# A four-sublayer decoder trunk on one core: the program is ordered by the scheduler's timeline simulation instead of its default one

## The chip, the cores and the metric

The kernel runs on one core of a Trainium2 chip. A core has five engines, each with its own queue, which it works off strictly in order: PE (TensorE: matrix multiplications; the load of its stationary operand is listed apart as PEld), DVE (VectorE: elementwise), ACT (ScalarE: elementwise with function tables), POOL (GpSimd) and SP (SyncE), which in this kernel issues all transfers between memory and the core. An engine that must wait for another waits on a semaphore, and everything behind that instruction in its queue waits too. The metric is the device time of one execution in microseconds (us).

## The reference

The reference does one inference step of a small hybrid decoder in fp32 for 512 prompt tokens and 64 sample tokens (8 sequences of 8), which share the weights. The model width is 1024. What is computed, cut to its core:

```
x += even_mixer(rmsnorm(x))   # conformer convolution + sliding-window attention (softmax with sinks)
x += conv_ffn(rmsnorm(x))     # silu(causal_conv3(h @ w_gate)) * (h @ w_up) @ w_down
x += odd_mixer(rmsnorm(x))    # Mamba-2: in-projection, conv4, chunked SSD scan, silu(z) gate, group RMS norm, out
x += conv_ffn(rmsnorm(x))
# the SSD scan of one head (32 heads in 4 groups, chunks of 128 tokens):
decay  = exp(where(causal, acum[l] - acum[s], -inf))
y_diag = ((C @ B.T) * decay * dt) @ x          # inside a chunk
states = B.T @ (decay_end * dt * x)            # what a chunk adds to the state
y_off  = (C @ h_prev) * exp(acum)              # what the earlier chunks bring
y = rmsnorm_group((y_diag + y_off + D * x) * silu(z)) @ w_out
```

The new states, caches and convolution histories are outputs too.

## The kernel before

The 576 tokens lie in the free dimension, in two halves of 288, with channels on the partitions. Every projection goes through `mm3` (lines 173 to 175): an fp32 product is made of three products of rounded parts (high by high, low by high, high by low), so each 128x128 block of weights against a half of the tokens costs three matrix multiplications of 288 columns. These three lines are 10,080 of the 11,007 multiplications that stand in PE's queue. Weights come in tiles of up to 1024 columns through rings of three buffers: the transfer lands in `wr`, ACT makes the rounded part `wh` (line 163), DVE the remainder `wl` (line 164).

The program goes through four sublayers in turn: `mix0` (convolution and attention), `ffn` 0, `mix1` (Mamba-2), `ffn` 1. In `mix1` the scan is written group by group as a generator `ssd(g)`, g = 0 to 3, and `run` weaves the projections of other parts between its steps, so that PE has multiplications (called **fillers** below) to do while a group's chains go from engine to engine. The chains of a group are:

- `xde` (DVE) to the state products `pst` (line 1081, PE; two pairs a group) to the states `hst` (lines 1087 to 1090), which free the two `xde` tiles of the pair.
- `decays(r)` for each of eight heads: the tile `acb` is loaded by SP (line 1112), goes through four Relu (line 1116) and one Exp (line 1117) on ACT and a multiplication by the mask on DVE (line 1118). The masks are forced into the order of the heads by a manual dependency.
- `outputs(t)` for four pairs of heads: 16 small multiplications `yp` (line 1148) take two `acb` tiles; `carried(t)` makes `py` (line 1133) for the same pair. DVE adds both into `xs` (lines 1152 and 1153).
- `begin`, `turn`, `finish`: the sample tokens, with `pyo` (line 1170) from loaded states `h0`, a transpose (line 1187), products `pst` (line 1200) and the outgoing states (lines 1203 and 1204).
- `gate(g)`: Silu of z (line 1262), products with it (1266), squares, the group norm through `rstd` (line 202: `pt`; a square root and DVE steps; line 218: `pr`), the scaling (1270) and the split into `yh`, `yl` (193, 194), on which the out-projection of the group works.

Tiles on the chip come from a list of 48 and later 59 slots (`S` and `free`). Which slot a tile gets is settled while the program is written down, in that order, and not by the scheduler. So an `acb` tile can only be loaded when the tile that had its slot before is done: in group 2, `acb_10552` takes the slot of `xde_10378` of the second state pair, `acb_10560` that of `hst_10415`, `acb_10680` that of `acb_10560`, `acb_10688` that of `ea2_10504`.

The order on each engine comes from the framework's scheduler. It simulates the program and, whenever a simulated engine comes free, gives it the instruction that it takes to be ready, earlier written ones first. A few places are bound by hand (`keep_in_program_order`, `issue_after`, the masks). The time at which the simulation believes an operand to be ready thus decides which of several waiting instructions goes ahead in a queue; on the chip the queue is then fixed.

## Time and profile before

| what | value |
|---|---|
| time, median of 3 runs | 1554.57 us (1550.0 to 1555.12) |
| the profiled execution's own time | 1553.1 us |
| its span in the profile | 1551.3 us |
| PE busy in the span | 1520.5 us (98%) |
| DVE, ACT, POOL busy | 1018.5, 649.3, 154.7 us |
| mean granted clock of PE | 0.997 of full speed |

The profile's page gives each engine's busy time, the longest chain of work, the groups of instructions by line, and the transfers. By time, `mix0` takes the first 195 us, `ffn` 0 until about 630 us, `mix1` until about 1,130 us (its groups end near 785, 905, 1,025 and 1,100 us), and `ffn` 1 the rest. A row of a timeline begins with the start in us and the duration in us; the bracket at its end gives the idle time before it and what ended it.

### The profile page before, as it was taken

The numbers are of one execution on the slowest core, as the hardware profiler recorded it, in microseconds if no ns is written. First come the engines' busy times: TensorE is split into PE (matmuls) and PEld (weight loads), VectorE is DVE, ScalarE is ACT, GpSimd is POOL, SyncE is SP. The second block draws the span as 40 slices with busy tenths as digits, with TensorE's granted clock in tenths as the row PEclk, the third lists the DMA queues.
The fourth block names the chain that finished last, engine by engine and source line by source line (L and its number), as shares of the span: only waits on it lengthen the run. The fifth ranks groups of instructions, "written<-read, shape, count | busy, mean of one in ns | idle before, by whom it ended". The sixth has DMA issues, their size and how long they took to land.

```text
span 1551.3 us, 28549 instructions
## 1 busy us (share of the span) xinstructions
PE 1520.5 (98%) x11635; PEld 1449.8 (93%) x11635; DVE 1018.5 (66%) x1805; ACT 649.3 (42%) x1232; POOL 154.7 (10%) x365
## 2 busy tenths in 40 slices
PE   8999999999999999999999999999999999999999
PEld 7977799999999999898988988998999999999999
DVE  7969887553555464678896786777976644663552
ACT  6356553221222222486855654646632222321220
POOL 0036001000000000011211112102010000000000
PEclk9999999999999999999999999999999999999999
DMA  8515223222222222136245245245222222223222
GB/s 239 136 42 131 85 70 98 86 86 85 83 77 78 92 82 85 55 104 202 71 148 180 83 115 185 72 125 173 87 84 85 91 83 82 82 73 92 82 87 75
DMA packets 69938, 157.80 MB, mean 102 GB/s; under 512 B 19871, under 2 KB 24607, under 8 KB 69807
## 3 DMA queue, kind: packets, MB, share of 16 engines
q1 hardware_dynamic: 69806, 155.97, 33.2%
q8 instruction: 92, 1.51, 0.4%
q14 instruction: 40, 0.32, 0.1%
HBM read 140.73 MB, written 15.21 MB: 101 GB/s over the span
## 4 chain that ended last, share of the span: by engine, by line
PE 88%; DVE 5%; ACT 4%; DMA 2%; issue 1%; SPq 0%; ACTq 0%; DVEq 0%
PE mm L173 27%; PE mm L175 27%; PE mm L174 26%; DMA acb<-acd 2%; PE yp L1148 1%; DVE wl L164 1%; ACT acb L1116 1%; PE mm L594 1%; ACT wh L163 1%; PE pst L1081 1%; PE pt L1063 1%; ACT sm L661 1%; PE py L1133 1%; PE pst L1200 1%; DMA out_ssm_s<-h 1%
## 5 line engine op out<-in xcount | busy, mean ns | idle before, releaser
L173 PE MATMUL mm<-hh,wh 128*128 128x288 f32 x2272 | 677.8, 299 | 6.8 <-ACT wh L163 5.5
L174 PE MATMUL mm<-hl,wh 128*128 128x288 f32 x2272 | 673.9, 297 | 0.7 <-DVE hl L389 0.4
L175 PE MATMUL mm<-hh,wl 128*128 128x288 f32 x2272 | 673.3, 297 | 0.5 <-DVE wl L164 0.4
L163 ACT ACTIVATE wh<-wr 128x1024 fp32r<-128x1024 f32 (+2 forms) x215 | 223.3, 1039 | 544.6 <-PE mm L174 275.1
L173 PEld LDWEIGHTS mm<-hh,wh 128*128 128x128 f32 x2272 | 428.3, 189 | 16.0 <-ACT wh L163 6.0
L174 PEld LDWEIGHTS mm<-hl,wh 128*128 128x128 f32 x2272 | 429.0, 189 | 4.8 <-issue 1.8
L175 PEld LDWEIGHTS mm<-hh,wl 128*128 128x128 f32 x2272 | 428.7, 189 | 3.2 <-issue 1.4
L164 DVE TENSOR_TENSOR wl<-wr,wh 128x1024 fp32r<-128x1024 f32 (+2 forms) x215 | 258.6, 1204 | 73.0 <-ACT wh L163 71.4
L173 PE MATMUL mm<-yh,wh 128*128 128x288 f32 x960 | 285.9, 298 | 1.5 <-DVE x L288 1.4
L175 PE MATMUL mm<-yh,wl 128*128 128x288 f32 x960 | 284.2, 297 | 1.3 <-DVE wl L164 1.3
L174 PE MATMUL mm<-yl,wh 128*128 128x288 f32 x960 | 285.3, 297 | 0.0
L173 PEld LDWEIGHTS mm<-yh,wh 128*128 128x128 f32 x960 | 181.1, 189 | 5.7 <-DVE x L288 2.5
L175 PEld LDWEIGHTS mm<-yh,wl 128*128 128x128 f32 x960 | 181.1, 189 | 2.4 <-DVE wl L164 1.6
L174 PEld LDWEIGHTS mm<-yl,wh 128*128 128x128 f32 x960 | 181.2, 189 | 1.5 <-issue 1.0
L288 DVE TENSOR_TENSOR x<-x,mm 128x288 f32<-128x288 f32 x192 | 84.9, 449 | 143.0 <-PE mm L175 142.8
L333 DVE TENSOR_TENSOR gbuf<-mm,rs 128x224 f32<-128x224 f32 x44 | 17.2, 391 | 108.6 <-PE mm L175 108.6
L344 ACT ACTIVATE gsilu<-gconv,par 128x512 f32<-128x512 f32 x44 | 31.8, 724 | 115.1 <-DVE gconv L341 115.1
L341 DVE SCALAR_TENSOR_TENSOR gconv<-gbuf,par,gconv 128x592 f32<-128x592 f32 x88 | 73.1, 831 | 1.5
L354 DVE TENSOR_TENSOR gsilu<-mm,gsilu 128x288 f32<-128x288 f32 x88 | 40.0, 454 | 50.5 <-PE mm L175 50.5
L880 DVE SCALAR_TENSOR_TENSOR cconv<-cbuf,par,cconv 128x600 f32<-128x600 f32 x72 | 59.6, 838 | 10.1 <-ACT cconv L878 9.5
L336 POOL COPY fpo<-gbuf 128x2 f32<-128x2 f32 x44 | 12.4, 281 | 476.0 <-DVE gbuf L333 476.0
L1116 ACT ACTIVATE acb<-acb,ac 128x128 f32<-128x128 f32 x128 | 41.4, 390 | 35.6 <-DMA acb<-acd 25.0
(322 smaller groups left out, 1593.6 us busy)
## 6 DMA issues: line engine op xcount, KB each, us to landing
wr<-in_w_gate SPq DMA_DIRECT2D x44, 512.0 KB, 3.5
wr<-in_w_up SPq DMA_DIRECT2D x44, 512.0 KB, 3.5
wr<-in_w_in_o SPq DMA_DIRECT2D x40, 512.0 KB, 3.6
wr<-in_w_down SPq DMA_DIRECT2D x32, 448.0 KB, 3.3
wr<-in_w_down SPq DMA_DIRECT2D x16, 512.0 KB, 3.5
h<-in_h SPq DMA_DIRECT2D x32, 256.0 KB, 3.1
acb<-acd SPq DMA_DIRECT2D x32, 256.0 KB, 4.2
out_ssm_s<-h SPq DMA_DIRECT2D x32, 256.0 KB, 2.6
```

What stands on the lines that cost most here:

```text
L163: nc.scalar.activation(hi[:, a:b], raw[:, a:b], AF.Copy)
L164: nc.vector.tensor_tensor(lo[:, a:b], raw[:, a:b], hi[:, a:b].bitcast(F32), op=SUB)
L173: nc.tensor.matmul(out, hi[:, ws], xh[:, sl], start=i == 0, stop=False)
L174: nc.tensor.matmul(out, hi[:, ws], xl[:, sl], start=False, stop=False)
L175: nc.tensor.matmul(out, lo[:, ws], xh[:, sl], start=False, stop=i == n - 1)
L288: nc.vector.tensor_tensor(self.x[m][:, sl], self.x[m][:, sl], p[:, :HB], op=ADD)
L333: nc.vector.tensor_tensor(g[:, 290:514], p[:, 0:224], rs[:, HB:NP], op=MUL)
L341: nc.vector.scalar_tensor_tensor(cv[:, :592], g[:, k:592 + k], w(k), cv[:, :592], op0=MUL, op1=ADD)
L344: nc.scalar.activation(sl[:, :NP], cv[:, :NP], AF.Silu, bias=b)
L354: nc.vector.tensor_tensor(sl[:, HALF[half]], p[:, :HB], sl[:, HALF[half]], op=MUL)
L880: nc.vector.scalar_tensor_tensor(cv[:, :600], g[:, k:600 + k], w(k), cv[:, :600], op0=MUL, op1=ADD)
L1116: nc.scalar.activation(acb[:, cs], acb[:, cs], AF.Relu, bias=ac[:, o:o + 1], scale=-1.0)
```

## The change

One argument is given where the program is traced. The scheduler then decides what is ready by its timeline simulation instead of its default one, for the whole program.

```
-    with tile.TileContext(nc) as tc:
+    with tile.TileContext(nc, schedule_with_timeline_sim=True) as tc:
         build(nc, tc, d)
```

The instructions of PE (11,007), DVE (1,807), POOL (370) and SP (436) are the same as before, with the same tiles in the same slots; ACT has 9 more, all of them loads of a function table (1,198 and 1,207 instructions). What changes is the order. `ffn` 0, `ffn` 1 and the end of the program are ordered nearly as before. The other parts are not. The table gives, for `mix1`, how many of the `mm3` multiplications stand ahead of an instruction in PE's queue, before and now. That is the measure in which the prediction counts fillers.

| | second `pst` pair (1081) | `yp` of the four pairs of heads | `pt`, `pt` / `pr`, `pr` of the group norm | out-projection begins |
|---|---|---|---|---|
| group 0 before | 4620 | 4608, 4656, 4704, 4752 | 4818, 4852 / 4865, 4915 | 4992 |
| group 0 now | 4728 | 4721, 4752, 4776, 4834 | 4944, 4974 / 4992, 4992 | 4992 |
| group 1 before | 5107 | 5132, 5174, 5225, 5280 | 5431 / 5468 (first ones) | 5664 |
| group 1 now | 5209 | 5226, 5280, 5301, 5328 | 5491 / 5515 (first ones) | 5664 |
| group 2 before | 5766 | 5798, 5835, 5883, 5952 | 6103 / 6140 (first ones) | 6336 |
| group 2 now | 5914 | 5928, 5952, 5971, 6029 | 6167 / 6195 (first ones) | 6336 |
| group 3 before | 6459 | 6528, 6575, 6592, 6605 | 6660, 6676 / 6678, 6714 | 6720 |
| group 3 now | 6564 | 6600, 6660, 6660, 6679 | 6720, 6720 / 6720, 6740 | 6720 |

In `mix0` the two `pt` and the two `pr` of the convolution's layer norm stood at 771 and 809, and 811 and 870, where the out-projection begins at 870; they stand at 849 and 859, and 864 and 866. Ahead of `mix1` the first `pr` of the norm (half 0) stood at 4210 and stands at 4224, where the first multiplication that needs it stands in both. At the very start ACT's first square (line 225) stands ahead of the first `wh` (line 163) and stood behind it. In group 3, SP loads the tiles of heads 4 to 7 ahead of those of heads 0 to 3, and the loads of `acb_11889` and `acb_11881`, on which the first `yp` waits, stand behind a load of weights (`wr_12607`) that stood after them.

First place: PE in group 2, just behind the second `yp`. (`py_10583` is the carried part of the third pair of heads, `pst_10628` and its like the sample's state products, `pyo` the sample's output from the loaded states `h0`, `mm` a filler.) Before:

```order
L1133 MATMUL py_10583<-cfm_9740,hst_10412 128x128
L1200 MATMUL pst_10629<-x3_10209,b3_10194 128x512
L173 MATMUL mm_10644<-yh_9645,wh_10590 128x288
L174 MATMUL mm_10644<-yl_9646,wh_10590 128x288
L175 MATMUL mm_10644<-yh_9645,wl_10591 128x288
L173 MATMUL mm_10644<-yh_9647,wh_10590 128x288
L174 MATMUL mm_10644<-yl_9648,wh_10590 128x288
L1200 MATMUL pst_10628<-x3_10209,b3_10194 128x512
```

Now:

```order
L1133 MATMUL py_10583<-cfm_9740,hst_10412 128x128
L1200 MATMUL pst_10629<-x3_10209,b3_10194 128x512
L1200 MATMUL pst_10628<-x3_10209,b3_10194 128x512
L1170 MATMUL pyo_10775<-h0_10678,cfm_9740 32x512
L1170 MATMUL pyo_10775<-h0_10676,cfm_9740 32x512
L1170 MATMUL pyo_10775<-h0_10674,cfm_9740 32x512
L1170 MATMUL pyo_10775<-h0_10672,cfm_9740 32x512
L1200 MATMUL pst_10636<-x3_10209,b3_10194 128x512
L1200 MATMUL pst_10637<-x3_10209,b3_10194 128x512
```

The fillers that stood between the small products have moved ahead of them, and `pyo_10775` has moved up; its `h0_10678` takes the slot of `acb_10552`, which the `yp` just before has read.

Second place: PE at the end of group 3, around the group norm and the start of the last out-projection (`mm_12453` to `mm_12481` are fillers of group 2's out-projection, `mm_12535` is the first product of group 3's, which needs `yh_12289` from the norm). Before:

```order
L174 MATMUL mm_12467<-yl_11029,wh_12449 128x288
L202 MATMUL pt_12357<-gssq_12287,o512_110 32x72 x4
L173 MATMUL mm_12481<-yh_11028,wh_12449 128x288
L174 MATMUL mm_12481<-yl_11029,wh_12449 128x288
L218 MATMUL pr_12328<-dg_12320,l1_75 128x288
L175 MATMUL mm_12453<-yh_11028,wl_12450 128x288
```

Now:

```order
L1133 MATMUL py_12118<-cfm_11125,hst_11778 128x128
L1133 MATMUL py_12118<-cfm_11125,hst_11780 128x128
L1133 MATMUL py_12118<-cfm_11125,hst_11850 128x128
L1187 MATMUL pt_12189<-ident_73,yo_12132 128x128 x4
L1200 MATMUL pst_12196<-x3_11604,b3_11585 128x512
L1200 MATMUL pst_12195<-x3_11604,b3_11585 128x512
L1200 MATMUL pst_12237<-x3_11604,b3_11585 128x512
L1200 MATMUL pst_12238<-x3_11604,b3_11585 128x512
L202 MATMUL pt_12315<-gssq_12287,o512_110 32x72 x4
L202 MATMUL pt_12357<-gssq_12287,o512_110 32x72 x4
L218 MATMUL pr_12328<-dg_12320,l1_75 128x288
L173 MATMUL mm_12535<-yh_12289,wh_12531 128x288
```

All fillers of group 2's out-projection now stand ahead of `py_12118`; behind it only the small products of the last group are left ahead of `mm_12535`.

Third place: ACT in `mix0`, where the softmax (line 661) alternates with the sigmoid of the convolution's gate (line 418). One piece of the difference:

```order
-L661 ACTIVATE sm,den<-sm,neg,rsq 128x128 x7
-L661 ACTIVATE sm,den<-sm,neg,rsq 128x256
+L661 ACTIVATE sm,den<-sm,neg,rsq 128x128 x5
+L418 ACT_TABLE_LOAD
+L418 ACTIVATE sg<-sg 128x288
+L163 ACTIVATE wh<-wr 128x1024
+L661 ACT_TABLE_LOAD
+L661 ACTIVATE sm,den<-sm,neg,rsq 128x256 x4
 L659 ACTIVATE es<-es 128x8
```

A sigmoid that stood behind the whole run of exponentials has moved into it, with a table load ahead of it and another one behind it. Over the part, the loads for these two lines go from 6 to 10.

## The prediction

> **What bounds the kernel now.** I read the page's head first, then the time by stages.
>
> ```profile
> span 1551.3 us, 28549 instructions
> PE 1520.5 (98%) x11635; PEld 1449.8 (93%) x11635; DVE 1018.5 (66%) x1805; ACT 649.3 (42%) x1232; POOL 154.7 (10%) x365
> 80.00:160.00 80.00, 77.64 (x649) 58.22 (x647) 62.38 (x178) 50.85 (x136) 38.42 (x39) 1.00 0.36 93
> 195.00:630.00 435.00, 435.00 (x3283) 434.24 (x3282) 242.32 (x398) 126.30 (x187) 17.82 (x83) 1.00 0.27 83
> 705.00:785.00 80.00, 79.25 (x618) 71.63 (x617) 68.61 (x117) 58.16 (x130) 17.49 (x32) 1.00 0.40 131
> 785.00:905.00 120.00, 115.31 (x887) 106.74 (x885) 90.71 (x151) 68.65 (x147) 19.83 (x33) 1.00 0.42 129
> 905.00:1025.00 120.00, 116.00 (x883) 107.64 (x882) 90.71 (x152) 69.36 (x148) 19.59 (x34) 0.99 0.41 127
> 1025.00:1095.00 70.00, 65.22 (x508) 57.07 (x509) 54.28 (x100) 40.25 (x89) 9.50 (x13) 1.00 0.46 142
> ```
>
> The window rows give length, then busy time and instructions of PE, PEld, DVE, ACT and POOL, the granted clock, and what the transfers did. PE is busy for 1520.5 of 1551.3 us. The change removes no multiplication, so no order can gain more than the 30.8 us in which PE is idle. In `ffn` 0 PE is never idle: 435.00 us over 3283 multiplications is 0.1325 us for a filler. In the groups of `mix1` the idle time is 0.75, 4.69, 4.00 and 4.78 us, 14.2 in all. Who ends it:
>
> ```profile
> PE yp L1148 <- DVE acb L1118: 7.2, 5, 2.4
> PE pst L1200 <- ACT ysb L1191: 1.9, 2, 1.3
> PE pr L218 <- DVE dg L214: 1.6, 3, 1.2
> PE mm L173 <- DVE x L288: 1.4, 2, 1.1
> ```
>
> (Us in total, times, longest.) So PE waits above all for the decay tiles. The kernel is fast because fillers cover chains through SP, ACT and DVE; the question is what the new order does to that cover.
>
> **The price of a chain.** Two waits of before, followed in time on PE:
>
> ```profile
> 920.44 1.91 PE L1081 MATMUL pst<-xde,btok 128*128 128x512 f32 x4
> 926.91 1.07 PE L1170 MATMUL pyo<-h,cfm 128*32 128x512 f32 x8
> 928.37 1.09 PE L1148 MATMUL yp<-acb,xdt 128*64 128x128 f32 x16
> 929.39 0.94 PE L1133 MATMUL py<-cfm,hst 128*128 128x128 f32 x6
> 934.70 0.60 PE L1187 MATMUL pt<-ident,yo 128*128 128x128 f32 x4
> 936.49 1.09 PE L1148 MATMUL yp<-acb,xdt 128*64 128x128 f32 x16 [0.80 <-DVE acb L1118]
> 948.21 1.97 PE L1148 MATMUL yp<-acb,xdt 128*64 128x128 f32 x16 [2.42 <-DVE acb L1118]
> ```
>
> These are group 2's second state pair and its first three `yp`. From the end of the state pair (922.35) to the second `yp` (936.49) are 14.1 us: **chain P2**, since its `acb` tiles take slots of that pair's `xde` and `hst`. From the end of the second `yp` (937.58) to the third (948.21) are 10.6 us: **chain P1**, since one tile takes the slot of the tile just read. Both are true lengths, because PE stood waiting at their ends. As a test of the counting: before, 48 fillers (6.4 us), `py` (0.9) and `pst` (1.5) stand between the second and third `yp`, which leaves a wait of 1.8 us; the row shows 2.42. Between pair and second `yp` stand 69 fillers (9.1) and 4.5 us of small products: a wait of 0.5 us by count; the row shows 0.80. What P1 is made of, the chain of waits shows for group 3:
>
> ```profile
> 1054.54 1.05 PE yp L1148 x16
> 1055.59 5.30 DMA acb<-acd
> 1061.00 1.57 ACT acb L1116 x5
> 1062.57 0.53 ACT acb L1117
> 1063.12 0.88 DVE acb L1118
> 1064.03 1.27 ACT acb L1116 x4
> 1066.37 1.09 DVE acb L1118
> 1067.50 1.09 PE yp L1148 x16
> ```
>
> There it takes 11.9 us. Moving fillers on PE shortens none of these pieces, except that the load of 5.30 us stood among others: the page gives
>
> ```profile
> acb<-acd SPq DMA_DIRECT2D x32, 256.0 KB, 4.2
> ```
>
> With 4.2 us P1 is 10.8. I take 10.6; the ends are 8 (an estimate: one tile alone, with the load of 4.2, four Relus of 1.27, an Exp of 0.6, the mask of 1.1 and the gaps between) and 12.
>
> **The change in `mix1`.** The state pairs now stand about 100 fillers later, and the four `yp` of a group closer together. A wait is the chain less what stands inside it on PE.
> - Group 0: from the state pairs (4728) to the second `yp` (4752) stand 24 fillers (3.2 us), the second pair (1.9), two `py` (1.8) and `pyo` (1.1), 8.0 with the rest of the first `yp`; P1 leaves 2.6. To the third `yp` (4776) 24 fillers (3.2) and 3.9 of small products leave 3.5. The fourth, 58 fillers on, has its cover. At 4992, where out-projection 0 begins, both `pr` now stand directly ahead of it, and what follows a `pr` is open (rows below): about 4. Sum 10.1.
> - Group 1: 71 fillers (9.4) and 4.6 of small products cover P2 (5209 to 5280). To the third `yp` 21 fillers (2.8) and 3.0 leave 4.8; the fourth 0.6. Sum 5.4.
> - Group 2: 38 fillers (5.0) and 4.6 leave 4.5 of P2 (5914 to 5952); to the third `yp` 19 fillers (2.5) and 3.0 leave 5.1 of P1; inside it also lies the wait of `pyo_10775` for its load. The fourth, 58 fillers on, is covered. Sum 9.6.
> - Group 3: the first `yp` stands 36 fillers (4.8) and 1.9 of small products behind the second pair. Its tiles take slots of `xde` tiles of both pairs, and their loads now stand behind a load of weights on SP: 7.4 by P2, 3.9 by P1; I take 7.4. The second `yp`, 60 fillers on (8.0 and `py`), waits 1.7. Then the norm. Its chain before, from DVE and ACT:
>
> ```profile
> 1078.64 0.75 DVE L1152 SCALAR_TENSOR_TENSOR xs<-xs,par,yp 128x512 f32<-128x512 f32 x1
> 1084.40 1.19 DVE L1266 TENSOR_TENSOR xs<-xs,zs 128x288 f32<-128x288 f32 x3
> 1087.56 1.28 ACT L209 ACT_TABLE_LOAD   x1
> 1088.85 0.32 ACT L209 ACTIVATE rv<-pt,eps 128x72 f32<-128x72 f32 x1
> 1091.50 0.45 DVE L214 TENSOR_TENSOR dg<-rv,rsc 128x288 fp32r<-128x288 f32 x1
> 1092.44 0.41 ACT L220 ACTIVATE grs<-pr 128x288 f32<-128x288 f32 x1 [0.46 <-PE pr L218]
> 1093.62 1.37 DVE L1270 SCALAR_TENSOR_TENSOR xs<-xs,par,grs 128x288 f32<-128x288 f32 x3
> 1094.16 1.30 ACT L193 ACTIVATE yh<-xs 128x288 fp32r<-128x288 f32 x3 [1.15 <-DVE xs L1270]
> ```
>
> From the products with z (1084.40) to the first `yh` (about 1094.6) are 10.2 us, from the last `yp`'s addition 16.0. Before, more than 100 fillers lay beside it; now none is left behind `py_12118`, whose sum into `xs` (1 us) comes ahead of that chain. I take 11, between 8 (only the last tile's products remain) and 16 (all of it). The step from `grs` to the third `yh` (1092.44 to 1095.46), 3 us a half, is also group 0's 4. Sum of group 3: 20.1.
>
> Together 45.2. The old waits on `yp` and `pst` (7.2 + 1.9 = 9.1) are what these replace: net **+36.1**.
>
> **The change elsewhere.**
> - Attention. ACT there, in three stretches, and what a table load costs:
>
> ```profile
> 100.00:110.00 10.00, 9.66 (x68) 7.96 (x67) 4.62 (x17) 9.45 (x27) 5.55 (x8) 1.00 0.00 0
> 110.00:120.00 10.00, 9.78 (x72) 8.62 (x71) 5.20 (x24) 9.07 (x23) 6.10 (x7) 1.00 0.26 68
> 120.00:130.00 10.00, 10.00 (x67) 7.66 (x64) 9.74 (x23) 8.70 (x27) 6.39 (x6) 1.00 0.72 188
> L418 ACT ACT_TABLE_LOAD x3 | 3.8, 1283 | 0.1
> 105.20 1.28 ACT L418 ACT_TABLE_LOAD   x1
> 106.49 0.78 ACT L418 ACTIVATE sg<-sg 128x288 f32<-128x288 f32 x2
> ```
>
> ACT is busy for 27.2 of 30 us and gets four more loads of 1.283 us: 5.1 on 2.8 of free time, so **+2.5**; 0 if PE's fillers cover the delay, 5.1 if ACT sets the pace. The other five of the nine loads lie where ACT is busy about half the time (68.65 of 120): nothing, unless one falls into a chain above.
>
>   The Trainium skill ("ScalarE: Activation LUTs", section "What ACT_TABLE_LOAD costs") adds a drain of about 1.38 us to each load, 2.66 us a switch. By the rows above the next instruction starts 1.29 us after the load began; no drain shows. By the page the four switches would cost an estimated 10.6 us of ACT.
>
> - Layer norm of `mix0`: 11 fillers (1.5 us) instead of 61 stand behind its last `pt`. From the table load to `grs` the rows above show 5.3 us (1087.56 to 1092.85), of which 1.5 are now covered: **+4** (0 to 5).
> - Ahead of `mix1` the first `pr` loses 14 fillers: **+2** (0 to 2). At the start 0.67 us of ACT (the square) go ahead of the first `wh`: **+0.6**.
> - Clock. After the wait of 2.42 us PE ran at half speed:
>
> ```profile
> 944.00:948.00 4.00, 1.79 (x14) 1.56 (x12) 2.45 (x3) 3.94 (x9) 0.00 (x0) 0.99 0.65 192
> 948.00:951.50 3.50, 3.29 (x23) 2.96 (x24) 0.91 (x2) 1.27 (x5) 0.00 (x0) 0.52 0.81 260
> ```
>
> At 0.52 these 3.29 us of work cost 1.6 more. Seven of the new waits are that long; where another wait follows within a few us, the slow stretch lies inside its chain. I count three: **+4.8** (0 to 8).
>
>   The Trainium skill ("TensorE: Matmul & The Clock Gate", section "What's actually happening") puts the fall to half clock behind an idle window of about 3.4 us; here 2.42 us sufficed. That window runs freely, so by the page only a wait of twice its length surely holds a whole one: of the new waits the two of group 3 alone, for 3.2 us in place of 4.8, and the sum would be 1598.
>
> - The waits for `dg` and `x` (1.6 + 1.4) stand at places where the order is new. I let them vanish: **-3.0**.
>
> Sum: 36.1 + 2.5 + 4 + 2 + 0.6 + 4.8 - 3.0 = 47.0 us on the profiled execution's 1553.1 (the median is 1554.57, 0.1% above): **1600 us**.
>
> **Rivals.**
> - *The same sign, less.* With P1 at 8 and P2 at 11.5 (both 2.6 shorter) the waits of the `yp` shrink by 17.8 (2.6 each, and the 0.6 and 1.7 to nothing); the tail at 8 saves 3, the clock term falls to 1.6: 1553 + 23 = 1576; with the terms outside `mix1` covered as well, 1567. For it: the chains share ACT with `wh` conversions and SP with weights, and fewer of these stand inside the shorter gaps. Against: 10.6 and 11.9 are the only two true lengths of P1 here.
> - *Faster.* The mechanism: in the old order an instruction that is early in the queue but late on the chip holds up PE although fillers stand behind it. If the new simulation's times are nearer to the chip's, the state products and `yp` come late in the queue because they truly are late, and the fillers moved ahead of them fill what was idle. It decides if the `acb` tiles land before the `yp` reach the queue's head, that is, if the loads lie ahead by more than the gaps of 19 to 24 fillers. Then the groups' 14.2 us of idle time go, and 4 of group 3's tail come back: 1553 - 10 = 1543. Against: the tiles that the third `yp` needs take the slots of those that the second one reads, so no simulation can load them earlier.
> - *No change that shows.* Early `yp` of a group are late by as much as the fillers moved ahead gain, and the tail of group 3 is hidden by DVE's other delays: 1555. That the argument does nothing is excluded: the order differs on every engine.
> - *The drain.* A drain of 1.4 us behind each load, which a row with a busy ACT could still show: four times 1.4 in attention, 5.5 us on top: 1606.
>
> **How the numbers follow.** Forecast 0.70, less of the same sign 0.14, faster 0.08, no change 0.05, drain 0.03. A change under 0.3% (4.7 us) can't be told from none. Slower by more than that is 0.70 + 0.14 + 0.03 = 0.87. The range: upwards, group 3's tail at 16 (+5), P1 at 12 (seven waits, +10), attention at 5.1 (+2.6), the clock at 8 (+3) and places that I didn't price make +40 at most, so 1640; downwards the second case to its end and a little below, 1559. Outside lie the 0.08, most of the 0.05 and some 0.05 above: 0.18.
>
> **What would show it.** Right: in the waits of the changed kernel, `yp` on `acb` rises from 7.2 to about 25 us, in single waits of 2.5 to 7 at the second and third `yp`; PE idles 8 us or more ahead of the first product of group 3's out-projection; `ffn` 0 keeps its 435 us; attention loses a few us. Wrong: if the `yp` wait stays under 10 us, the slot chains are shorter than I read them, and if PE's idle time falls below 30.8 us, the faster case holds. The table of stages tells how the loss splits: I expect 7 to 9 us ahead of `mix1` and the rest in it, two thirds of that in groups 0 and 3.

## The result and the profile after

| | before | after |
|---|---|---|
| time, median of 4 runs each on one chip | 1552.77 us (1550.0 to 1555.12) | 1624.67 us (1622.33 to 1627.54) |
| span of the profiled execution | 1551.3 us | 1620.1 us |
| PE busy, PE idle in the span | 1520.5, 30.8 us | 1548.5, 71.6 us |
| time at half clock between the start and the end | 10.2 us | 71.7 us |
| mean granted clock of PE | 0.997 | 0.978 |

The ratio is 1.0468, with a 95% interval of 1.0452 to 1.0483: the change costs 72 us, where 47 were forecast. The direction and the range (1559 to 1640) held, and the size was 25 us short.

The head of the changed kernel's page:

```profile
span 1620.1 us, 28588 instructions
PE 1548.5 (96%) x11635; PEld 1466.6 (91%) x11635; DVE 1017.4 (63%) x1805; ACT 658.8 (41%) x1241; POOL 166.5 (10%) x365
```

The span grew by 68.8 us: 40.8 of it is more idle time of PE, and 28.0 is busy time, although the multiplications are the same 11,635 records. About 24 of those 28.0 us are work done at half clock (51.8 us of busy time in the stretches at half clock against 10.0, and 9.6 against 3.6 ahead of the first record of full clock; half of both differences). The stages (length, then busy time and instructions of PE, PEld, DVE, ACT, POOL, the granted clock, and the transfers; the cuts lie at about the same places in the program as the rows of before, though not to the instruction):

```profile
207.00:642.00 435.00, 435.00 (x3284) 434.46 (x3284) 241.12 (x396) 125.69 (x185) 15.71 (x83) 1.00 0.27 82
720.00:813.00 93.00, 79.58 (x580) 67.12 (x579) 72.30 (x121) 60.74 (x135) 24.39 (x32) 0.95 0.44 131
813.00:934.00 121.00, 115.29 (x840) 105.58 (x840) 85.54 (x149) 63.12 (x136) 18.72 (x31) 0.94 0.37 115
934.00:1057.00 123.00, 114.17 (x854) 104.25 (x854) 86.51 (x147) 63.60 (x139) 20.76 (x32) 0.97 0.38 120
1057.00:1163.00 106.00, 88.43 (x641) 77.74 (x640) 68.56 (x115) 53.09 (x111) 12.57 (x19) 0.90 0.42 128
```

`ffn` 0 keeps its 435.00 us to the hundredth. The groups of `mix1` have PE idle for 13.4, 5.7, 8.8 and 17.6 us up to 1163, against 0.75, 4.69, 4.00 and 4.78, and each runs below full clock.

PE has the same 10,080 fillers to do, so the cleanest ledger counts by filler: how much later the n-th one starts after than before, read from the two traces, against the terms of the forecast for that place. (Small products that now stand elsewhere count where they stand.)

| place (fillers) | later by, us | in this place | forecast |
|---|---|---|---|
| `mix0` (up to 1000) | 12.1 | 12.1 | 7.1 (attention 2.5, layer norm 4, start 0.6) |
| ahead of `mix1` (to 4445) | 13.7 | 1.6 | 2 |
| group 0 (to 5033) | 33.3 | 19.6 | 10.1 - 0.6 of old waits = 9.5 |
| group 1 (to 5543) | 38.8 | 5.5 | 5.4 - 3.4 = 2.0 |
| group 2 (to 6336) | 45.7 | 7.0 | 9.6 - 3.2 = 6.4 |
| group 3 (to 6800) | 68.9 | 23.1 | 20.1 - 1.9 = 18.2 |
| the rest | 68.8 | 0 | 0 |

The forecast column sums to 45.2; with -3.0 for waits taken to vanish and 4.8 for the clock it is the 47.0 on record. Idle time of PE alone grew by 12.4, 1.3, 4.8 and 16.3 us in these four groups; what is lost beyond that is slower work. Who ends PE's waits (us in total, times, longest):

```profile
PE mm L173 <- ACT zs L1251: 7.3, 4, 5.6
PE mm L173 <- ACT wh L163: 6.6, 2, 5.8
PE pt L202 <- DVE gssq L229: 6.2, 2, 3.5
PE pyo L1170 <- DMA h<-in_h: 5.9, 3, 2.4
PE yp L1148 <- DVE acb L1118: 5.3, 1, 5.3
...
PE pr L218 <- ACT grs L220: 3.5, 1, 3.5
...
PE mm L173 <- ACT ch L193: 3.3, 1, 3.3
```

This is the surprise of the trace. I had said that `yp` on `acb` would rise from 7.2 to about 25 us. It fell to 5.3. The first row (5.8 us of the second row are the start, where before 5.4 were) is a *filler* that waits for ACT to copy z out of the accumulator that the filler needs.

**Group 0's tail**, the place that was missed by most. PE, and then ACT, at the norm of group 0 (start, duration; the bracket is the idle time before it and what ended it):

```profile
801.83 0.66 PE L1006 MATMUL pt<-ident,bfm 128*128 128x128 f32 x4 [1.59 <-ACT rv L209]
803.49 0.40 PE L218 MATMUL pr<-dg,l 128*128 128x288 f32 x1 [1.01 <-DVE dg L214]
807.36 0.61 PE L218 MATMUL pr<-dg,l 128*128 128x288 f32 x1 [3.47 <-ACT grs L220]
```

```profile
794.26 1.28 ACT L209 ACT_TABLE_LOAD   x1
...
795.89 1.28 ACT L882 ACT_TABLE_LOAD   x1
...
800.16 1.28 ACT L209 ACT_TABLE_LOAD   x1
...
804.50 1.28 ACT L882 ACT_TABLE_LOAD   x1
805.80 0.72 ACT L882 ACTIVATE xs<-cconv,par 128x512 f32<-128x512 f32 x1
806.92 0.39 ACT L220 ACTIVATE grs<-pr 128x288 f32<-128x288 f32 x1
```

While group 0's norm goes through its two halves, ACT works at the convolution of the next group (lines 878 to 882). The norm wants the square root, the convolution the Silu, so ACT loads four tables in 11.5 us, and `grs` stands behind the last of them and a Silu. The second `pr` needs the accumulator that `grs` empties, so PE stands for 3.47 us. Fillers 4900 to 5033 take 13.5 us more; my term for this was 4. Of the 13.5 us 7.6 are waits, about 1 is small products that stood ahead of filler 4900 before, and the rest is work in a stretch of 13.7 us at half clock.

**Group 3.** ACT, and the filler on PE that waits for it:

```profile
1112.42 2.65 ACT L1116 ACTIVATE acb<-acb,ac 128x128 f32<-128x128 f32 x8 [1.45 <-DMA acb<-acd]
...
1117.32 0.69 ACT L1251 ACTIVATE zs<-mm 128x288 f32<-128x288 f32 x2
```

```profile
1117.77 0.61 PE L173 MATMUL mm<-yh,wh 128*128 128x288 f32 x1 [5.61 <-ACT zs L1251]
...
1154.98 0.74 PE L1200 MATMUL pst<-x,b 96*128 96x512 f32 x2 [1.94 <-DVE h L1203]
1158.44 0.47 PE L202 MATMUL pt<-gssq,o 128*32 128x72 f32 x8 [2.72 <-DVE gssq L229]
1162.43 0.47 PE L202 MATMUL pt<-gssq,o 128*32 128x72 f32 x8 [3.53 <-DVE gssq L229]
...
1165.26 0.85 PE L173 MATMUL mm<-yh,wh 128*128 128x288 f32 x2 [1.53 <-ACT yh L193]
```

ACT's queue holds the Relus (1116) ahead of the copies of z (1251). The Relus wait for their load, the copies wait behind them, and the filler that was to cover the decay chain waits for the copy. The wait is the decay chain's, but it shows one step earlier than I had put it. Together with 2.09 us for `x` just before, it is 7.7 us; the forecast for the first `yp` was 7.4. The tail, from `pst` to the first product of the out-projection, has waits of 1.04, 1.94, 2.72, 3.53, 0.23 and 1.53 us, 11.0 together; the forecast was 11.

**Group 2, where the chains were priced.** PE and DVE from the second `yp` to the third:

```profile
995.80 1.97 PE L1148 MATMUL yp<-acb,xdt 128*64 128x128 f32 x16 [5.34 <-DVE acb L1118]
1002.19 1.92 PE L1170 MATMUL pyo<-h,cfm 128*32 128x512 f32 x8 [1.87 <-DMA h<-in_h]
1005.48 1.21 DVE L1118 TENSOR_TENSOR acb<-acb,cbm 128x512 f32<-128x512 f32 x1
1008.72 1.09 PE L1148 MATMUL yp<-acb,xdt 128*64 128x128 f32 x16
```

The second state pair ends at 981.67, so P2 is 14.1 us again, and its wait shows at the second `yp`. P1 is not 10.6: the tiles of the third `yp` are ready at 1006.69, 8.9 us behind the second one, and PE, which was held up by `pyo` in the meantime, comes to the third `yp` 2 us after that. No wait is left there.

**`mix0`.** The same stretches before and after:

```profile
120.00:140.00 20.00, 20.00 (x135) 15.69 (x132) 19.47 (x40) 15.24 (x41) 15.11 (x13) 1.00 0.57 156
140.00:160.00 20.00, 19.04 (x158) 15.08 (x156) 19.14 (x45) 9.46 (x25) 8.51 (x8) 1.00 0.59 142
180.00:200.00 20.00, 19.60 (x151) 18.98 (x150) 19.74 (x44) 15.59 (x34) 1.37 (x8) 1.00 0.34 111
```

```profile
120.00:140.00 20.00, 20.00 (x139) 16.20 (x137) 15.41 (x41) 19.92 (x50) 12.82 (x14) 1.00 0.50 132
140.00:160.00 20.00, 17.97 (x121) 11.64 (x117) 18.15 (x42) 12.99 (x34) 15.74 (x13) 0.91 0.69 170
180.00:200.00 20.00, 16.11 (x126) 14.88 (x124) 17.77 (x40) 12.67 (x24) 2.09 (x6) 1.00 0.37 105
```

From 120 to 140 us ACT is busy for 19.92 of 20 us with the added table loads, and PE still has no gap: its fillers cover them. The loss lies at three other places. At the start there are 2.1 us of waits for the first norm, which now comes late, and the first record of full clock comes at 15.8 us in place of 9.3; at the 300th filler 1.4 us of lag are left. Little of that is the order's: of six executions below whose `mix0` has the order of before, five show full clock first at 13.3 to 14.9 us, and those five are 0.7 to 1.2 us late at the 50th filler. At the 850th filler the lag is 6.2 us, with a wait of 1.75 us and a stretch at half clock at the end of attention; the rest of this step doesn't show as a wait. At the layer norm it goes from 6.2 to 12.1 (3.5 us more idle, and a stretch at half clock).

### The profile page after: what moved, and what is told of

Read it like the earlier page. It is cut to its first block, busy times and chain, and to the rows that moved or that the text cites. A ratio compares the mean times of both kernels' runs of the same rounds, so it can differ in the third digit from the quotient of the medians.

```text
span 1620.1 us, 28588 instructions
## 1 busy us (share of the span) xinstructions
PE 1548.5 (96%) x11635; PEld 1466.6 (91%) x11635; DVE 1017.4 (63%) x1805; ACT 658.8 (41%) x1241; POOL 166.5 (10%) x365
## 4 chain that ended last, share of the span: by engine, by line
PE 87%; DMA 5%; DVE 4%; ACT 3%; issue 1%; SPq 0%; ACTq 0%; DVEq 0%
PE mm L173 26%; PE mm L174 26%; PE mm L175 26%; DMA acb<-acd 2%; PE mm L594 1%; PE yp L1148 1%; DMA h<-in_h 1%; PE sc L682 1%; ACT acb L1116 1%; PE pyo L1170 1%; DMA es<-acd 1%; DMA ea<-acd 1%; PE pst L1081 1%; DVE wl L164 1%; ACT wh L163 0%
## 5 line engine op out<-in xcount | busy, mean ns | idle before, releaser
L173 PE MATMUL mm<-hh,wh 128*128 128x288 f32 x2272 | 678.2, 299 | 11.4 <-ACT wh L163 6.6
L173 PE MATMUL mm<-yh,wh 128*128 128x288 f32 x960 | 288.5, 302 | 13.4 <-ACT zs L1251 5.6
L1176 POOL TENSOR_TENSOR h<-h,cds 128x512 f32<-128x512 f32 x32 | 39.6, 1266 | 230.3 <-PE pyo L1170 230.3
```

The source lines that it names most:

```text
L173: nc.tensor.matmul(out, hi[:, ws], xh[:, sl], start=i == 0, stop=False)
L1176: nc.gpsimd.tensor_tensor(hp(h0[bh][b4]), hp(h0[bh][b4]), cds[:, b * 32 + 8 * g:b * 32 + 8 * g + 8].unsqueeze(2).broadcast_to([P, 8, 64]), ...
```

## The experiments

All of them use the same tool. Behind `build`, a table lists instruction numbers engine by engine, and each listed instruction is bound to come behind the one listed before it. That fixes an engine's order without adding any wait between engines; what is not listed is ordered by the default scheduler.

```
         build(nc, tc, d)
+        chain(nc, tc)
...
+def chain(nc, tc):
+    ...
+        i = by["I-%d" % at]
+        if prev is not None:
+            tc.add_manual_dep(i, prev, mybir.DependencyInfo(
+                mybir.DependencyClass.NoSync, mybir.DependencyReason.DATA), reason="as listed")
+        prev = i.name
```

The theory on record is called A: the loss adds up from chains that lost their cover, place by place, on PE's idle time. The kernel before had medians of 1550.05, 1551.6 and 1552.16 us beside the three sets of runs.

### One part of the program at a time

```
+ORDER = "..."   # e1: every engine as now up to the end of mix0, as before behind it
+ORDER = "..."   # e2: every engine as now in mix1, as before ahead of it
+ORDER = "..."   # e3: every engine as now in group 3, as before ahead of it
```

> Each engine's order is fixed by a list: up to the middle of ffn 0 the order of the changed program, from there on the order of before; nothing is left out. Theory A (each part's order costs its own share, read from the two traces by the time at which the same filler starts: +12.0 us at the 2,000th filler): 1565 us, +10 to +14. Theory B (what a part loses is caught up or made worse by what follows): outside of that, with the rest of the program not at before's pace.

> The order of before up to the 4,445th filler (just before group 0 of mix1), from there on the order of the changed program. Theory A: the rest of the loss, 68.8 - 13.7 = 55 us: 1608 us, +50 to +60. Theory B: clearly less, since the groups then start from before's state of buffers and weights.

> Only group 3 of mix1 in the changed program's order (from the 6,264th filler to the middle of ffn 1), all else in the order of before. Theory A: 68.8 - 45.7 = 23 us: 1576 us, +20 to +26. Theory B (group 3 suffers from what groups 0 to 2 left late): +5 to +15.

| | median, us | ratio (95%) | expected | filler ledger |
|---|---|---|---|---|
| `mix0` alone | 1560.34 | 1.0060 (1.0044 to 1.0076) | 1565 | +11.2 at the end of `mix0` |
| `mix1` alone | 1610.31 | 1.0368 (1.0337 to 1.0398) | 1608 | +57.6 at the end |
| group 3 alone | 1574.64 | 1.0147 (1.0123 to 1.0171) | 1576 | +21.8 at the end |

The parts are nearly independent: 9 + 57 = 66 of the 72 us by the ratios (10 + 60 by the medians), and group 3 alone costs the 23 us that it costs in the whole. The first number came out at the lower edge of its expectation (+10 to +14), and the trace says why. The 11.2 us are there at filler 4224, as in the changed kernel, but behind it 8.5 us came back, most of them at the three places where the kernel before had stretches at half clock and this execution had none. The executions of this kernel spread from 1555.8 to 1564.5 us with one and the same order, those of the kernel before from 1547.9 to 1557.4.

### Which engine's order costs it

```
+ORDER = "..."   # e4: PE alone, as now
+ORDER = "..."   # e5: ACT, DVE, POOL and SP, as now; PE not listed
```

> Only PE's order is that of the changed program, from start to end; the default scheduler orders ACT, DVE, POOL and SP around it. Theory A1 (PE's order is the cause: fillers stand where they cover nothing): +55 to +75 us, 1608 to 1628. Rival A2 (the queues of ACT and SP are the cause, which let loads and copies stand behind one another): +25 or less, 1578 or less.

> The counterpart of the run with PE's order alone: ACT, DVE, POOL and SP have the changed program's order, and the default scheduler orders PE around them. Theory A1 (PE's order is the cause): most of the loss goes, +0 to +25 us, 1550 to 1575. Rival A2 (the other queues are the cause): +45 or more, 1595 or more.

Measured: 1641.21 us (1.0576, 1.0551 to 1.0601) with PE's order alone, 1633.43 us (1.0523, 1.0506 to 1.0541) with the other four. The reading that PE's order does it and the other engines only follow has fallen: both sides bring the whole loss alone, and more of it than both together. A fixed order on one side makes the default scheduler arrange the other side around it, so these two kernels are not the change minus a half of it. What they show is that the lists fit each other better than either fits a remainder made around it; what each side's order costs by itself they leave open.

### Is it the half clock?

28 of the 68.8 us are more busy time, most of it at half clock. If that time were a cost of its own, keeping PE busy in its waits should win much of it back. Products on a constant operand, whose results are overwritten before anything reads them, are put ahead of the waiting instruction at 15 places (100 products, and in a second kernel 64; its expectation below says 61). They add work that computes nothing.

```
+WARM = {12: 10, 82: 5, 85: 6, 89: 3, ...}
+    def warm(self, out):
+        ...
+        for _ in range(WARM.get(k, 0)):
+            m = self.nc.tensor.matmul(out[:, 0:P], self.ident, self.o512, start=True, stop=True)
...
+        self.warm(pt)
```

> The changed program, every engine in its order, with 100 multiplications added that compute nothing used: they write into a bank of PSUM just before its real product does, and stand on PE at 15 of its waits (3 to 16 of them, for about the length of each wait). Theory C (28 us of the loss is PE at half clock after windows that are mostly idle, not the waits themselves): about 11 of the 15 windows' worth of slow work go, 1.7 us each: 15 to 20 us faster than the changed kernel, 1605 to 1610. Rival D (the slow records are a mark of the waits and cost nothing of their own, since PE waits anyway): 1624 or more, as what is added can only lengthen.

> The changed program with added products that keep PE busy in its waits, as the first of this kind, but 61 instead of 100 of them, fewer where they stood longer than the wait (state products and pyo of group 0, the yp of group 2, the group norm of group 3). Theory C' (half clock costs something, and the first try gave it back by overlong filling): 4 to 10 us faster than the changed kernel, 1614 to 1620. Rival D (half clock lies inside chains of other engines and costs nothing): 1622 or more.

| | median, us | span, us | half clock between start and end, us | mean clock |
|---|---|---|---|---|
| changed kernel | 1624.67 | 1620.1 | 71.7 | 0.978 |
| 64 products | 1630.03 (1.0500, 1.0477 to 1.0523) | 1627.1 | 58.0 | 0.982 |
| 100 products | 1623.79 (1.0466, 1.0449 to 1.0484) | 1619.7 | 23.9 | 0.992 |

In the profiled execution two thirds of the half clock went (by the mean clocks of the other three, 0.986 to 0.988, about half), and the time stayed. That this way of filling the waits wins back 15 to 20 us has fallen. The first product on group 0's `yh` in the kernel with 100 products (its line numbers are a little higher, since lines were added):

```profile
810.37 0.40 PE L179 MATMUL mm<-yh,wh 128*128 128x288 f32 x1 [1.15 <-ACT yh L199]
```

In the changed kernel it started at 810.86, so the chain over DVE and ACT that it waits for ends at nearly the same time. From filler 4900 to 5033 the stretch at half clock is 3.4 us here and 13.7 there, and this part takes 31.5 us here and 33.0 there: 10 us less of half clock were worth 1.5 us beside this chain. At other places more came back and was lost again. At filler 4445 this execution is 3.5 us ahead of the changed one, and up to filler 4900, where 14 of the added products stand, it loses 3.0.

So these runs don't show that half clock is free, and others speak against it. The 34 executions of the kernel before that were timed beside the runs have one and the same order: at mean clocks of 0.999 and 1.000 they took 1547.9 to 1550.5 us, at 0.993 to 0.996 they took 1553.5 to 1557.4. The four of the changed kernel go from 1622.3 us at 0.978 to 1627.5 at 0.973. A longer wait can lengthen the time and lower the clock at once, so this shows that the two go together, and not which sets the other.

### Is it the copies of z behind the Relus?

By the trace, 14 copies of z stand behind Relus that wait for loads. They were moved ahead of them on ACT; nothing else is changed. One piece:

```
-L1116 ACTIVATE acb<-acb,ac 128x128 x4
-L1251 ACTIVATE zs<-mm 128x288
+L1251 ACTIVATE zs<-mm 128x288
+L1116 ACTIVATE acb<-acb,ac 128x128 x4
```

> The changed program with PE, DVE, POOL and SP in its order; on ACT 14 copies of z (line 1251), each of which frees the bank that a filler needs, stand up to 11 instructions earlier, ahead of Relus and Exps of the decays that wait for their loads. Theory F (part of the loss in mix1 is that fillers can't run beside the chain, because their copies queue behind the decays on ACT: waits of 5.6 and 0.8 us and the fillers that then follow the chain): 6 to 14 us faster than the changed kernel, 1610 to 1619. Rival G (the chain over the loads decides, so PE then waits at the yp instead): 1622 or more.

Measured: 1635.94 us (1.0539, 1.0516 to 1.0563), 11 us *slower* than the changed kernel, where this theory had put 6 to 14 us less. Its waits on PE:

```profile
PE yp L1148 <- DVE acb L1118: 9.4, 5, 2.6
...
PE pt L1187 <- DVE ea L1137: 5.4, 2, 4.6
...
PE ysp L1235 <- DVE yo L1180: 4.3, 2, 4.1
```

The waits of the fillers for z have fallen from 7.3 to 4.0 us in all, and the `yp`, the transpose and the sample's products wait in their place. On ACT the copies now stand idle for what they need themselves (line 1251 in the groups by line: busy, mean ns, then the idle time ahead of them and who ended it), in the changed kernel and in this one:

```profile
L1251 ACT ACTIVATE zs<-mm 128x288 f32<-128x288 f32 x32 | 12.2, 396 | 5.1 <-PE mm L175 5.0
```

```profile
L1251 ACT ACTIVATE zs<-mm 128x288 f32<-128x288 f32 x32 | 12.4, 403 | 43.6 <-PE mm L175 19.3 <-DMA out_ssm_s<-h 16.9 <-DMA out_ssm_p<-hst 3.3
```

A copy of z waits for its product on PE, and by this row also for outgoing states whose transfers must end first. Put ahead, the copies waited 43.6 us in all at the head of ACT's queue, in place of 5.1, and the Relus behind them. So moving one step of a late chain moved the wait into others, which is what the rival had said of the `yp`. It doesn't show what the copies cost where they stood: this far ahead they held up ACT themselves. A place between the two was not tried.

### The cover of group 3's tail, alone

From the order of before, the last 22 small products of group 3 are put 60 fillers later on PE. That takes away cover as the change does. The other engines are not listed, so the default scheduler orders them around it; by the trace the order of ACT, DVE and SP differs from before in places, most of them at this tail.

```
+ORDER = "..."   # e7: as before, PE's last yp, py, pt and pst of group 3 sixty fillers later
```

> PE's order of before but for one place: the 22 small products from the last yp of group 3 up to its group norm stand 60 fillers later (at most directly ahead of the last out-projection), as in the changed program; the other engines are ordered by the default scheduler around it and differ only there. Theory E (the tail of group 3 costs what it has lost in cover: 16 us from the last yp, of which 55 fillers or 7.3 us still lie beside it): 7 to 9 us of waits and 2 to 5 of clock, +9 to +14, 1560 to 1565. Rival (the tail waits for DVE and ACT, which get to it sooner when nothing else is asked of them): +4 or less.

Measured: 1558.94 us (1.0053, 1.0032 to 1.0074), 8 us slower; the expectation by lost cover was 9 to 14, its rival at most 4. The tail's waits are 2.44, 2.15, 0.50 and 0.83 us, 5.9 together, where 7 to 9 were worked out, and a stretch of 10.2 us at half clock lies beside them. From filler 6264 to 7500 this execution loses 6.7 us on the one before. So lost cover on PE costs less here than the counting said and more than its rival, and it is about a third of the 23 us that group 3 costs in the change.

### The other direction

Four waits of before (1.66, 0.41, 0.80 and 2.42 us at `yp`) come from small products that stand a little too early in PE's queue. They were moved behind 14 more fillers in group 1, and behind 7 and 27 more in group 2; in a second kernel also up to 7 in group 3. One piece of the first:

```
+L173 MATMUL mm<-hh,wh 128x288
+L174 MATMUL mm<-hl,wh 128x288
+L175 MATMUL mm<-hh,wl 128x288
 L1148 MATMUL yp<-acb,xdt 64x128 x8
 L1133 MATMUL py<-cfm,hst 128x128 x3
```

> The order of before on every engine, but on PE the small products of group 1 from the second yp on stand 14 fillers later, and those of group 2 7 and then 27 fillers later; 100 small products are moved. Theory (the waits of before at these places are fillers that stand on the wrong side of a yp): the waits of 1.7, 0.4, 0.8 and 2.4 us and one window at half clock (1.7) go, 4 to 7 us faster than before, 1543 to 1546. Rival (the chain to the next yp starts later by as much, and what is gained is given back): no change.

> As the run with the small products of groups 1 and 2 later on PE (1545.6 us), and in addition those of group 3 from the second yp on up to 7 fillers later (the last yp stays where it is). 138 small products are moved; all other engines are in the order of before. Theory: the wait of 1.9 us at that yp falls by 0.9 us: 1544 to 1545.5. Rival (the end of group 3 starts later by as much): 1545.6 or a little more.

Measured: 1545.61 us (0.9959, 0.9947 to 0.9972) and 1544.13 us (0.9953, 0.9937 to 0.9969). Both beat the kernel before by 6 to 8 us, 0.4 to 0.5%, and the changed one by 79 to 81; between the two the intervals leave no difference. The first one's page and its waits at `yp` (7.2 us before):

```profile
span 1544.1 us, 28549 instructions
PE 1518.6 (98%) x11635; PEld 1448.5 (94%) x11635; DVE 1018.7 (66%) x1805; ACT 648.7 (42%) x1232; POOL 154.7 (10%) x365
```

```profile
PE yp L1148 <- DVE acb L1118: 2.9, 3, 1.9
```

PE's idle time falls from 30.8 to 25.5 us, and the stretch at half clock in group 2 is gone, as is the one ahead of `mix1`; the 1.9 us are group 3's and were there before.

### Table loads in attention, alone

In the order of before, two sigmoids are put among the exponentials, as the change does it, which makes four more table loads. One piece:

```
 L661 ACTIVATE sm,den<-sm,neg,rsq 128x128 x7
+L418 ACT_TABLE_LOAD
+L418 ACTIVATE sg<-sg 128x288
+L661 ACT_TABLE_LOAD
 L661 ACTIVATE sm,den<-sm,neg,rsq 128x256
```

> The order of before on every engine, but for two sigmoids (line 418) on ACT that stand among the exponentials of the softmax, as in the changed program: four more table loads, 5.1 us of ACT in a stretch in which 2.8 us were free. By the sum of the prediction +2.5 us (0 to 5.1): 1554 on a before of 1551.6. By a drain of 1.4 us behind each load +8: 1559. Rival: nothing, PE's fillers cover it.

Measured: 1563.22 us (1.0074, 1.0055 to 1.0092), 11.4 us slower, where loads alone gave 0 to 5.1. ACT, and PE's wait behind it:

```profile
103.31 0.44 ACT L418 ACTIVATE sg<-sg 128x288 f32<-128x288 f32 x1 [4.81 <-DVE sg L417]
103.77 1.28 ACT L661 ACT_TABLE_LOAD   x1
105.07 0.60 ACT L661 ACTIVATE sm<-sm,neg,rsq 128x256 f32<-128x256 f32 x1
```

```profile
112.73 1.98 PE L704 MATMUL po<-ptb,vt 128*64 128x512 f32 x4 [3.92 <-ACT ptb L701]
142.23 0.65 PE L699 MATMUL pt<-ident,sm 128*128 128x128 f32 x4 [3.67 <-ACT ptb L701]
```

The experiment did not isolate what it should. The sigmoid came to the head of ACT's queue before DVE had its operand, and everything behind it stood for 4.81 us (and for 1.11 us at the second sigmoid). Most of the 4.81 us are not new, since in the kernel before ACT stood idle at the same place:

```profile
100.29 0.60 ACT L661 ACTIVATE sm<-sm,neg,rsq 128x256 f32<-128x256 f32 x1 [3.94 <-DVE neg L657]
```

On PE the two waits above are 7.3 us longer than the waits at these places before (0.34 us and none). The other part is the clock: in this stretch PE has three windows at half clock (from 112.6, 143.4 and 157.0 us, 3.4 us each, nearly all busy, so 1.7 us of work lost in each), and the kernel before has none. 7.3 and 5.1 are 12.4 us; by the ledger attention loses 12.2. In the changed kernel, where PE's order moved along, its loads cause no wait up to 140 us (the row from 120 to 140 us above). No drain shows: the exponential starts 1.30 us after its load began, with the load itself 1.28. Of the 121 table loads in the traces of the kernel before, the changed one and this one, 107 have ACT's next instruction start 1.29 to 1.30 us after they began; at the other 14 it waits for DVE or PE.

## Why the prediction was right, and where it was short

- **The mechanism held in the main.** Chains that had more than enough fillers beside them lost them, the losses add up by place, and `ffn` 0 and `ffn` 1 are untouched. The forecast of PE's idle time was 42.2 us of growth (47.0 without the clock's 4.8); it grew by 40.8. By group of `mix1` it grew by 12.4, 1.3, 4.8 and 16.3 us, where 9.5, 2.0, 6.4 and 18.2 were forecast, so part of the sum's nearness is luck: misses of both signs cancel.
- **Group 2, the two chains P1 and P2.** The second `yp` waits 5.34 us, where P2 less its cover gave 4.5, and P2's length carried over to a tenth of a us. P1's did not: from the second `yp` to the tiles of the third it was 10.0, 10.0 and 8.9 us in groups 0, 1 and 2, where 10.6 was taken, and the waits of 3.5, 4.8 and 5.1 us at the third `yp` did not come. Other waits of PE stood in the same gaps (1.2, 3.7 and 2.3 us). That group 2 lost 7.0 us, where 6.4 were forecast, is thus partly luck. The trace of before could have told: its group 1 has two more steps that end in a wait at a `yp` (1.66 and 0.41 us), and they are 8.5 and 9.0 us long, so 10.6 and 11.9 were not the only lengths.
- **The step from `grs` to the third `yh`, "3 us a half, is also group 0's 4", failed for group 0.** Group 0 has 7.6 us of waits there in place of 4, and with slow work and moved products lost 13.5; group 3's tail has the 11.0 of waits that were forecast. I had taken the norm's pieces from a place where ACT has nothing else to do. In group 0 the next group's convolution shares ACT, with another function table, and a norm of two halves goes through the switch twice.
- **"In the waits, `yp` on `acb` rises from 7.2 to about 25 us" was wrong.** It is 5.3 us. By my own test ("if the `yp` wait stays under 10 us, the slot chains are shorter than I read them") that would be the chains' length alone. P1 was indeed 0.6 to 1.7 us shorter, but that does not explain 20 us. The test was badly chosen: a filler needs an accumulator that ACT must have emptied, and ACT's copies stand in one queue with the decay chain. So the same lateness shows at fillers, at `pyo` and at the norm as well. By place group 2 stayed near the forecast; group 1 lost 5.5 us, where 2.0 were forecast, with 10.2 us at half clock in it.
- **Attention +2.5 was mis-sized, by its place.** The loads are hidden up to 140 us. The 12.1 us of `mix0` are 1.4 at the start (0.6 forecast), 4.8 from there to the end of attention (2.5), and 5.9 at the layer norm, whose 4 us were 3.9 of waits (0.59 and 3.30) before the half clock behind them.
- **The clock, +4.8, was mis-sized.** The sum for idle time came out, and the busy time grew by 28.0 us, about 24 of them at half clock. So by bookkeeping the term that fell short is this one; I had counted three slow windows, and there were 18 more than before. Whether it is also the cause of the missing 25 us stays open. Where PE is busy a slow window goes with 1.7 us of lost work and the time is longer by as much (the run with table loads alone); beside the chain of group 0's norm 10 us less of half clock gained 1.5. I can't split the 25 us between the two.
- **-3.0 for the waits on `dg` and `x`** did not come: 2.3 and 4.4 us now stand where 1.6 and 1.4 were.
- **The two thirds.** Groups 0 and 3 hold 42.7 of the 55.2 us of `mix1`, 77%; ahead of `mix1` 13.7 us were lost, where 7 to 9 were expected.
- **The rivals.** "Less of the same sign" and "no change" are out by the time. "Faster" was wrong for this change, though its mechanism is real: small products that stand too early do hold up PE, and moving them behind 7 to 27 fillers gained 6 to 8 us. The simulation moved them by about 100. "The drain" does not show in any of the 121 table loads of three traces.

What stays open: why the simulation believes those operands to be late was not tried; nor was the whole change with attention's order alone undone, nor a layout with more slots for the `acb` tiles. Whether moving copies, loads and Relus together would bring the changed order back is not known.

## What to carry to other kernels

Cover is not a number of fillers on PE: each filler needs what other engines free for it, and a chain that is late on ACT takes the fillers with it, so price a chain by its place and not by the instruction at which you expect the wait. Where two parts with different function tables meet on one engine, take the length of a step from that very meeting and not from a quiet place. And where a trace shows small products waiting with fillers right behind them, moving them by as many fillers as the wait is long, and no more, is worth a trial: here it beat both kernels, by half a per cent against the one before.

## What the runs showed of the hardware

The clock's records lie on a grid of 3.413 us, and the clock changes only at its lines: the stretches at half clock are 1 to 4 such windows long in these two traces, and up to 5 in the other runs'. Around two of them, one in the kernel before and one in the changed kernel (the clock is the figure ahead of the last two):

```profile
944.53:947.94 3.41, 1.26 (x10) 1.03 (x8) 2.39 (x3) 3.38 (x9) 0.00 (x0) 1.00 0.56 159
947.94:951.35 3.41, 3.14 (x22) 2.81 (x23) 0.96 (x2) 1.18 (x5) 0.00 (x0) 0.50 0.86 264
```

```profile
800.90:804.30 3.40, 1.05 (x5) 0.60 (x5) 2.42 (x5) 2.97 (x8) 0.34 (x1) 1.00 0.00 0
804.30:807.70 3.40, 0.34 (x1) 0.34 (x2) 1.63 (x4) 3.38 (x8) 0.88 (x2) 0.50 0.53 136
```

A window need not be empty: the clock fell behind windows in which PE was busy for 37% and 31%. Over both traces it fell behind windows busy for up to 59%, and some windows busy for 47% to 54% brought no fall. In the other twelve traces there are falls behind windows busy for 71% and 72% (the run with table loads alone, and the second one with small products later). So the busy share of the window just before does not settle it alone. At half clock it came back behind windows busy for 83% or more, but three times it stayed at half behind a window that was busy throughout. The page "TensorE: Matmul & The Clock Gate" of the Trainium skill, section "What's actually happening", speaks of an idle window of about 3.4 us; the length agrees, the idleness does not.

Where the lines of the grid fall in the program differs from execution to execution, and so do the slow windows: the kernel with `mix0` alone changed took 1555.8 us at a mean clock of 0.998 and 1564.5 at 0.993, with one order. What a slow window costs depends on its place. In the run with table loads alone, three in busy stretches go with 1.7 us each; beside a chain that PE waits for anyway, three fewer were worth 1.5 us together.
